# Opening and first sweep of a gated recurrence block: loads in written order, three products of the first unit over six row pairs first, side work tied to its units

## The chip, the cores and the metric

The kernel runs on one core of one Trainium2 chip. The metric is device time in microseconds (us) for one execution, lower is better. The engines are named as in the profile: PE (matrix products), PEld (its weight loads), DVE (vector), ACT (scalar), POOL (GpSimd), SP (the engine that issues most loads).

## What is computed

The block works on 1024 positions of 2048 channels. A conditioning vector gives a shift, a scale and a gate for each channel; the normalised input, scaled and shifted, is projected to eight parts (`w_in`) and to two merge gates (`w_merge`); a recurrence and a short convolution use the parts; two up-projections, a merge and a last projection follow.

```python
mod = jnp.einsum('bd,de->be', silu(c), w_ada[l]) + b_ada[l]
shift, scale, gate = (m[:, None, :] for m in jnp.split(mod, 3, axis=-1))
h = rms_norm(x, g_pre[l]) * (1.0 + scale) + shift
proj = jnp.einsum('bsd,de->bse', h, w_in[l])            # 8 parts of 1024 columns
...
merge = jax.nn.sigmoid(jnp.einsum('bsd,de->bse', h, w_merge[l]) + b_merge[l])
out = jnp.einsum('bsd,de->bse', m_a * p_a + m_b * p_b, w_o[l])
x = x + gate * rms_norm(out, g_post[l])
```

All weights and activations are 32-bit floats.

## The kernel before

**Products.** Each large product is made by a seven-product scheme over 2 x 2 blocks (p1 to p7), and each factor is split in a high and a low part, so that one row pair `g` of one product costs three matmuls of 128x128 by 128x512 (L118, L121, L122 in `mm3`). One product over eight row pairs is 24 matmuls. The split of a weight block is one ACT cast (`w_hi`, L129) and one DVE subtraction (`w_lo`, L130); that of an activation block is the same on half the size (L134, L135).

**Opening (`ph0`).** Sixteen loads bring x, the rows are normalised and transposed on PE into `xT` (L204). Then `ada_pair(q)`, for q from 0 to 3, forms shift and scale of 512 channels each: eight steps of two 512 KB loads, one of the scale weights that PE multiplies (`prow`, L234, two fp32 matmuls for each load, which the profile shows as four records) and one of the shift weights that DVE accumulates (`row_v`, L236 and L238). Every third of these 64 loads lands in a ring of four buffers of its own (`ada`), the others in the large pool `big` (38 slots of 4 KB per partition). At the end of each q, PE turns the two rows into columns (`pa`, L243), and DVE makes `a_c` and `sh_c` of them (L246 to L248). `factors_a` applies them to `xT` for two row pairs at a time and writes the split factors `fa` of p1, p6, p2 and p7. Row pairs 6 and 7 need the columns of q = 3, so they come last.

**First sweep (`ph1`).** 48 units; a unit loads four weight blocks (`w_raw`, 512 KB each, a ring of five buffers shared with scratch of the opening), forms s1, s2 and s4 on DVE, stores s1 and s4 to `s_scr`, and runs the four products p1, p6, p2, p7: 96 matmuls. Its result `o` is stored to `u_scr`. Unit 0 runs p1 and p6 over row pairs 0 to 5 first, in an order written out by hand (L341 to L344). Beside the units run three kinds of side work that no product of this sweep needs: `factors_b` (factors of the second sweep, written after units 0, 2 .. 14), `gate_step` (the gate's 32 loads and its accumulation on DVE, after units 16 to 31) and `sums_o` (sums of blocks of `w_o`, four loads, four DVE operations and four stores each, after units 32, 34 .. 46).

**Order.** Apart from what is pinned by hand, a planner at compile time sets the order in which each engine issues its instructions: it simulates the program and hands an engine, whenever that is free, the earliest written instruction that is ready by its own times and has a buffer. On the chip that order is fixed, and each engine and each load queue goes through it one by one. `keep_in_program_order` ties an instruction behind the one written before it on the same engine. `issue_after` ties what is written in its block, on the engine of a given instruction, behind that one. A pool opened after another one is closed lies in the same memory; its tiles wait for the old tiles at their place.

Of the kernel before, what the change touches and what calls it, by code (L numbers as in the profile page):

```python
# [15 lines left out]
P = 128  # L16
# [10 lines left out]
def tile_hgrn2_shortconv_block(  # L27
# [105 lines left out]
    def split_h(t, raw, eng):  # L133
        eng(out=t[:, 0], in_=raw)  # L134
        nc.vector.tensor_sub(out=t[:, 1], in0=raw, in1=t[:, 0].bitcast(F32))  # L135
# [40 lines left out]
    def load_x(si):  # L176
        for q in range(2):
            t = bigt(F32, f"x_{si}_{q}")
            nc.sync.dma_start(out=t, in_=x[si * P:(si + 1) * P, q * S:(q + 1) * S])
# [75 lines left out]
    def factors_a(gs, vec=()):  # L255
# [14 lines left out]
        def keep_f(s, g, raw):  # L270
            fa[s][g] = pair(f"f{s}_{g}")
            split_h(fa[s][g], raw, nc.scalar.copy)
# [9 lines left out]
        for g, b11, b12, b21, b22 in parts:  # L282
            keep_f("p7", g, b12)
# [15 lines left out]

    for si in range(8):  # L300
# [18 lines left out]
    units = [(w_in_v, (2 * j) * 1024 + i * P, (2 * j + 1) * 1024 + i * P) for i in range(NH) for j in range(4)]  # L319
    units += [(w_merge_v, 256 * m, 256 * m + P) for m in range(16)]  # L320

    def load_q(view, par, e0):
        raw = wp.tile([P, 8, P], F32, tag="raw", name="w_raw", bufs=5)
        nc.sync.dma_start(out=raw, in_=view[:, par, :, e0:e0 + P])
        return raw

    def unit_a(u):
        view, e1, e2 = units[u]
        a11, a21 = load_q(view, 0, e1), load_q(view, 0, e2)
        a22, a12 = load_q(view, 1, e2), load_q(view, 1, e1)  # L330
        o = ph.tile([P, 3, HS], F32, tag="o", name="o", bufs=2)
        s1, s2, s4 = (ph.tile([P, 8, P], F32, tag=f"s{n}", name=f"s{n}") for n in (1, 2, 4))
        px, py = ps("mm", "px"), ps("mm", "py")
        w1 = split_w(a11)
        if u:
            product(px, w1, fa["p1"])
        nc.vector.tensor_add(out=s1, in0=a21, in1=a22)
        nc.vector.tensor_sub(out=s2, in0=s1, in1=a11)
        nc.gpsimd.dma_start(out=s_scr[u][:, 0], in_=s1.rearrange("p a b -> p (a b)"))
        w6 = split_w(s2)  # L340
        if u == 0:  # L341
            for gs in (range(6), (6, 7)):
                product(px, w1, fa["p1"], pin=True, gs=gs)
                product(py, w6, fa["p6"], pin=True, gs=gs)  # L344
        nc.scalar.copy(out=o[:, 2], in_=px)  # L345
        if u:
            product(py, w6, fa["p6"])
        nc.vector.tensor_add(out=o[:, 1], in0=o[:, 2], in1=py)
        nc.vector.tensor_sub(out=s4, in0=a12, in1=s2)
        nc.gpsimd.dma_start(out=s_scr[u][:, 1], in_=s4.rearrange("p a b -> p (a b)"))  # L350
        product(px, split_w(a12), fa["p2"], more=True)
        nc.scalar.copy(out=o[:, 0], in_=px)  # L352
        nc.vector.tensor_sub(out=a21, in0=a11, in1=a21)
        product(py, split_w(a21), fa["p7"], more=True)
        nc.vector.tensor_add(out=o[:, 2], in0=o[:, 2], in1=py)
# [588 lines left out]
```

## Time and profile before

| | us |
|---|---|
| median of 3 runs | 2783.63 (2783.16 to 2787.78) |
| the profiled execution | 2786.26 |
| its span, first to last instruction | 2784.6 |
| PE busy in it | 2670.7 (96%) |
| DVE busy | 1725.3 (62%) |
| ACT busy | 915.0 (33%) |

The profiled execution lies 2.63 us, a tenth of a per cent, above the median. A busy PE in this profile includes the pipelined overlap of matmuls, so the rate at which matmuls start says more than the busy share. Times in the rows are us from the start of the span, unless marked ns.

### The profile page before, as it was taken

To read this page: it belongs to the slowest core of one execution; us is meant where nothing else is said; L and a number is where in the kernel's file an instruction comes from. 1 tells how busy PE (TensorE), PEld (TensorE's weight loads), DVE (VectorE), ACT (ScalarE), POOL (GpSimd) and SP (SyncE) were. 2 spreads that over 40 slices of the span, in tenths; PEclk is the share of its full clock that TensorE was granted. 3 is DMA by queue.
4 is the path that set the end of the run, shared out by engine and by line. 5 is a ranking of instruction groups with operands and counts; after the bars stand their busy time and mean duration, and the time that the engine had idled before them with its cause. 6 is when DMAs were issued, how large, how long until landed. Compare 5 with 4: busy or idle time off the path is not lost.

```text
span 2784.6 us, 31067 instructions
## 1 busy us (share of the span) xinstructions
PE 2670.7 (96%) x11851; PEld 2152.5 (77%) x11851; DVE 1725.3 (62%) x2128; ACT 915.0 (33%) x1192; POOL 246.6 (9%) x431
## 2 busy tenths in 40 slices
PE   4899999999999999999999999999998999999997
PEld 3277787888888888888888878888886877878785
DVE  6887886755544455546565666653338678755668
ACT  4433222222222222234334444333334232232334
POOL 2011111110000000020000000000001101000000
PEclk9999999999999999999999999999999999999999
DMA  9769999985555556683433443357665547673254
GB/s 361 282 229 324 317 356 356 347 279 183 190 181 174 177 173 192 184 299 124 142 124 122 142 139 123 119 190 228 201 225 175 173 148 248 221 272 99 85 213 171
DMA packets 405990, 576.76 MB, mean 207 GB/s; under 512 B 17772, under 2 KB 280016, under 8 KB 405712
## 3 DMA queue, kind: packets, MB, share of 16 engines
q1 hardware_dynamic: 352640, 369.15, 43.0%
q0 software_dynamic: 52016, 201.42, 19.0%
q10 hardware_dynamic: 1184, 4.20, 0.4%
q8 instruction: 93, 1.52, 0.2%
q14 instruction: 57, 0.47, 0.0%
HBM read 405.87 MB, written 168.82 MB: 206 GB/s over the span
## 4 chain that ended last, share of the span: by engine, by line
PE 71%; issue 11%; DVE 7%; DMA 6%; ACT 3%; POOL 2%; DVEq 0%; POOLq 0%; ACTq 0%; SPq 0%
PE po L833 9%; PE py L122 6%; PE py L121 6%; PE px L122 6%; PE py L118 6%; PE px L118 6%; PE px L121 6%; PE pz L118 5%; PE pz L122 5%; PE pz L121 5%; PE pw L121 3%; PE pw L122 3%; PE pw L118 3%; DMA w_raw<-in_w_in_dram 2%; DVE w_lo L130 1%
## 5 line engine op out<-in xcount | busy, mean ns | idle before, releaser
L129 ACT CAST w_hi<-w_raw 128x1024 fp32r<-128x1024 f32 (+1 forms) x304 | 299.4, 985 | 1008.7 <-PE px L121 401.3
L130 DVE TENSOR_TENSOR w_lo<-w_raw,w_hi 128x1024 fp32r<-128x1024 f32 (+1 forms) x304 | 345.3, 1136 | 260.4 <-ACT w_hi L129 256.3
L122 PE MATMUL py<-fp,w_lo 128*128 128x512 f32 x768 | 302.4, 394 | 7.2 <-DVE w_lo L130 7.1
L122 PE MATMUL px<-fp,w_lo 128*128 128x512 f32 x768 | 300.3, 391 | 5.5 <-DVE w_lo L130 5.5
L118 PE MATMUL py<-fp,w_hi 128*128 128x512 f32 x768 | 300.9, 392 | 2.2 <-ACT o L352 1.3
L118 PE MATMUL px<-fp,w_hi 128*128 128x512 f32 x768 | 300.5, 391 | 0.5 <-ACT o L345 0.5
L121 PE MATMUL py<-fp,w_hi 128*128 128x512 f32 x768 | 300.6, 391 | 0.0
L121 PE MATMUL px<-fp,w_hi 128*128 128x512 f32 x768 | 299.5, 390 | 0.0
L833 PE MATMUL po<-w_hi,lt 128*128 128x512 f32 x896 | 244.7, 390 | 6.2 <-ACT lt L134 4.0
L833 PEld LDWEIGHTS po<-w_hi,lt 128*128 128x128 f32 x896 | 167.9, 188 | 44.1 <-ACT lt L134 4.8
L122 PEld LDWEIGHTS py<-fp,w_lo 128*128 128x128 f32 x768 | 145.3, 189 | 42.6 <-DVE w_lo L130 12.1
L129 ACT CAST w_hi<-s 128x512 fp32r<-128x512 f32 (+1 forms) x112 | 90.2, 805 | 267.9 <-PE py L121 242.4
L122 PEld LDWEIGHTS px<-fp,w_lo 128*128 128x128 f32 x768 | 144.4, 188 | 37.1 <-DVE w_lo L130 7.0
L118 PEld LDWEIGHTS py<-fp,w_hi 128*128 128x128 f32 x768 | 145.2, 189 | 33.0 <-ACT w_hi L129 3.0
L118 PEld LDWEIGHTS px<-fp,w_hi 128*128 128x128 f32 x768 | 144.6, 188 | 31.7 <-ACT o L345 0.9
L121 PEld LDWEIGHTS py<-fp,w_hi 128*128 128x128 f32 x768 | 145.2, 189 | 30.4
L121 PEld LDWEIGHTS px<-fp,w_hi 128*128 128x128 f32 x768 | 144.6, 188 | 30.5 <-issue 0.5
L118 PE MATMUL pz<-fp,hi 128*128 128x512 f32 x384 | 151.8, 395 | 0.0
L121 PE MATMUL pw<-fp,w_hi 128*128 128x512 f32 x384 | 151.4, 394 | 0.0
L118 PE MATMUL pw<-fp,w_hi 128*128 128x512 f32 x384 | 151.0, 393 | 0.0
L118 PE MATMUL pz<-fp,w_hi 128*128 128x512 f32 x384 | 150.4, 392 | 0.0
L122 PE MATMUL pw<-fp,w_lo 128*128 128x512 f32 x384 | 150.1, 391 | 0.0
(285 smaller groups left out, 4917.2 us busy)
## 6 DMA issues: line engine op xcount, KB each, us to landing
w_raw<-in_w_in_dram SPq DMA_DIRECT2D x160, 512.0 KB, 5.1
s_scr<-s POOLq DMA_DIRECT2D x96, 512.0 KB, 6.0
s_raw<-s_scr SPq DMA_DIRECT2D x96, 512.0 KB, 4.2
w_raw<-in_w_merge_dram SPq DMA_DIRECT2D x80, 512.0 KB, 5.7
u_scr<-o POOLq DMA_DIRECT2D x48, 768.0 KB, 7.4
ada_raw<-in_w_ada_dram SPq DMA_DIRECT2D x64, 512.0 KB, 10.8
d<-u_scr SPq DMA_DIRECT2D x48, 512.0 KB, 5.0
ga_raw<-in_w_ada_dram SPq DMA_DIRECT2D x32, 512.0 KB, 8.4
```

What stands on the lines that cost most here:

```text
L118: mm = nc.tensor.matmul(o, ah, bh, start=first, stop=False, skip_group_check=True)
L121: nc.tensor.matmul(o, ah, bl, start=False, stop=False, skip_group_check=True)
L122: nc.tensor.matmul(o, al, bh, start=False, stop=last, skip_group_check=True)
L129: nc.scalar.copy(out=hi, in_=raw)
L130: nc.vector.tensor_sub(out=lo, in0=raw, in1=hi.bitcast(F32))
L833: nc.tensor.matmul(o, a, b[:, c], start=st, stop=sp, skip_group_check=True)
```

## The change

All loads of the opening and the first sweep are issued in written order (`load`). The ring of the conditioning loads shrinks: every fifth of them, instead of every third, goes to a buffer of its own, and there is one such buffer instead of four; the others go to `big`. Unit 0 moves into the opening's pool: its four weight loads are written before those of q = 3, its splits and s1, s2 too (a generator that stops at `yield`), and a third split (p2's) joins them. After the last `ada_pair` and `factors_a`, its products p1, p6 and p2 run over row pairs 0 to 5 and then over 6 and 7, in written order, p2 in a PSUM tile of its own; its remaining DVE work is tied behind the last factor. Side work is written after other units: `factors_b` after units 2, 4 .. 16, `gate_step` after 10 to 25, `sums_o` after 26, 28 .. 40.

```diff
+    def load(o, i):
+        tc.keep_in_program_order(nc.sync.dma_start(out=o, in_=i))
...
-        if n_ada[0] % 3:
+        if n_ada[0] % 5:
             raw = bigt(F32, "ada_raw").rearrange("p (k e) -> p k e", k=2)
         else:
-            raw = ph.tile([P, 2, HS], F32, tag="ada", name="ada_raw", bufs=4)
-        nc.sync.dma_start(out=raw, in_=w_ada_v[:, k:k + 2, t, q * HS:(q + 1) * HS])
+            raw = ph.tile([P, 2, HS], F32, tag="ada", name="ada_raw", bufs=1)
+        load(raw, w_ada_v[:, k:k + 2, t, q * HS:(q + 1) * HS])
...
-        row_p, row_v = (ph.tile([P, HS], F32, tag=t, name=t) for t in ("row_p", "row_v"))
+        row_p, row_v = (ph.tile([P, HS], F32, tag=t, name=t, bufs=n) for t, n in (("row_p", 1), ("row_v", 2)))
...
+    def load_a(u):
+        view, e1, e2 = units[u]
+        return [load_q(view, *a) for a in ((0, e1), (0, e2), (1, e2), (1, e1))]
+
+    def unit_a(u, raws):
+        a11, a21, a22, a12 = raws
+        o = ph.tile([P, 3, HS], F32, tag="o", name="o", bufs=2 if u else 1)
+        s1, s2 = (ph.tile([P, 8, P], F32, tag=f"s{n}", name=f"s{n}", bufs=1) for n in (1, 2))
+        s4 = ph.tile([P, 8, P], F32, tag="s4", name="s4") if u else a22
+        px, py = ps("mm", "px"), ps("mm", "py")
+        v = nc.vector
+        w1 = split_w(a11)
+        if u:
+            product(px, w1, fa["p1"])
+        v.tensor_add(out=s1, in0=a21, in1=a22)
+        v.tensor_sub(out=s2, in0=s1, in1=a11)
+        nc.gpsimd.dma_start(out=s_scr[u][:, 0], in_=s1.rearrange("p a b -> p (a b)"))
+        w6 = split_w(s2)
+        if u == 0:
+            w2 = split_w(a12, out_t=(ph.tile([P, 8, P], F32R, name="hi3a", bufs=1), wp.tile([P, 8, P], F32R, tag="raw", name="lo3a", bufs=5)))
+            yield
+            p2 = ps("mm", "p2")
+            for gs in (range(6), (6, 7)):
+                for p, w, f in ((px, w1, "p1"), (py, w6, "p6"), (p2, w2, "p2")):
+                    product(p, w, fa[f], pin=True, gs=gs)
+        nc.scalar.copy(out=o[:, 2], in_=px)
...
     for q in range(1, 4):
+        if q == 3:
+            first = unit_a(0, load_a(0))
+            next(first)
         ada_pair(q)
         factors_a((2 * q - 2, 2 * q - 1))
-    factors_a((6, 7), vec=(7,))
+    with tc.issue_after(factors_a((6, 7), vec=(7,)).ins):
+        next(first, None)
     ph_pool.__exit__(None, None, None)
...
     for u in range(NU):
-        unit_a(u)
-        if u < 16:
-            if u % 2 == 0:
-                factors_b(u // 2)
-        elif u < 32:
-            gate_step(2 * u - 32)
-            gate_step(2 * u - 31)
-        elif u % 2 == 0:
-            sums_o((u - 32) // 2)
+        if u:
+            for _ in unit_a(u, load_a(u)):
+                pass
+        if u in range(2, 18, 2):
+            factors_b(u // 2 - 1)
+        if 10 <= u < 26:
+            gate_step(2 * u - 20)
+            gate_step(2 * u - 19)
+        elif u in range(26, 42, 2):
+            sums_o((u - 26) // 2)
```

The loads in `load_x`, `gate_step` and `sums_o` go through `load` as well. The second sweep's `load_q` stays unpinned.

## Rows read from the trace of the kernel before

**Rows 1.** The page, part 1: busy us (share of the span) and instructions.
```profile
PE 2670.7 (96%) x11851; PEld 2152.5 (77%) x11851; DVE 1725.3 (62%) x2128; ACT 915.0 (33%) x1192; POOL 246.6 (9%) x431
```

**Rows 2.** Stretches: length; PE, PEld, DVE, ACT, POOL busy (instructions); clock share; DMA share; GB/s.
```profile
108.00:138.13 30.13, 23.34 (x73) 7.10 (x73) 27.62 (x45) 14.08 (x22) 0.00 (x0) 0.94 0.82 304
138.13:169.05 30.92, 25.93 (x98) 19.86 (x98) 26.80 (x36) 12.60 (x19) 2.73 (x5) 0.89 0.56 168
190.00:250.00 60.00, 56.35 (x248) 46.02 (x247) 50.22 (x63) 23.02 (x33) 11.74 (x22) 1.00 0.86 292
250.00:500.00 250.00, 243.30 (x1048) 198.26 (x1047) 188.88 (x207) 58.09 (x69) 37.59 (x70) 0.99 1.02 344
600.00:1212.00 612.00, 611.82 (x2693) 504.07 (x2692) 299.39 (x277) 144.97 (x168) 52.33 (x98) 1.00 0.61 187
```

**Rows 3.** Timeline of PE in the opening: start, length, what, [idle before <-releaser].
```profile
44.68 12.18 PE L234 MATMUL prow<-ada_raw,c_act 128*1 128x512 f32 x28
71.99 3.27 PE L234 MATMUL prow<-ada_raw,c_act 128*1 128x512 f32 x4 [15.13 <-DMA ada_raw<-in_w_ada_dram]
...
137.21 1.05 PE L243 MATMUL pa<-ones,row_v 128*128 128x1 f32 x8
138.13 0.49 PE L118 MATMUL px<-fp,w_hi 128*128 128x512 f32 x1
```

**Rows 4.** Timeline of SP's load queue in the opening, merged by line.
```profile
0.81 14.42 SPq L179 DMA_DIRECT2D x<-in_x_dram  x16
...
24.53 9.92 SPq L324 DMA_DIRECT2D w_raw<-in_w_in_dram  x5
34.50 89.07 SPq L223 DMA_DIRECT2D ada_raw<-in_w_ada_dram  x60
```

**Rows 5.** DMA, 0 to 140 us in 40 slices; adaLN loads of 40 to 140 us.
```profile
GB/s 123 305 386 414 411 410 406 387 340 291 285 365 379 392 387 386 387 387 387 386 386 149 225 150 92 208 273 373 365 394 387 386 389 387 385 386 387 240 0 5
...
DMA to landing us min/median/max: 3.8/10.8/12.0
```

**Rows 6.** Timeline of DVE from the last conditioning step to the last factor.
```profile
135.62 1.54 DVE L238 SCALAR_TENSOR_TENSOR row_v<-ada_raw,c_act,row_v 128x512 f32<-128x512 f32 x2
...
141.98 0.81 DVE L265 TENSOR_SCALAR xT<-xT,a_c,sh_c 128x1024 f32<-128x1024 f32 x1
...
150.18 1.28 DVE L278 TENSOR_TENSOR xT<-xT 128x512 f32<-128x512 f32 x2
...
160.67 0.69 DVE L135 TENSOR_TENSOR fp<-xT,fp 128x512 fp32r<-128x512 f32 x1
```

**Rows 7.** Timeline of PE inside unit 0 and at its end.
```profile
147.22 0.80 PE L122 MATMUL py<-fp,w_lo 128*128 128x512 f32 x1 [3.07 <-DVE w_lo L130]
147.82 0.63 PE L118 MATMUL py<-fp,w_hi 128*128 128x512 f32 x1
148.24 0.63 PE L121 MATMUL py<-fp,w_hi 128*128 128x512 f32 x1
...
169.05 0.39 PE L118 MATMUL px<-fp,w_hi 128*128 128x512 f32 x1
```

**Rows 8.** Two stalls of PE in the sweep and what DVE did before them.
```profile
220.10 0.68 DVE L291 TENSOR_TENSOR xx<-fp 128x512 f32<-128x512 f32 x1
...
222.57 0.50 PE L122 MATMUL py<-fp,w_lo 128*128 128x512 f32 x1 [2.12 <-DVE w_lo L130]
...
270.04 1.23 DVE L337 TENSOR_TENSOR s<-w_raw 128x1024 f32<-128x1024 f32 x1 [3.17 <-DMA w_raw<-in_w_in_dram]
...
274.85 0.50 PE L122 MATMUL px<-fp,w_lo 128*128 128x512 f32 x1 [2.99 <-DVE w_lo L130]
```

**Rows 9.** DMA issues: KB each, median us to landing; 250 to 400, 600 to 1200, page.
```profile
w_raw<-in_w_in_dram SPq DMA_DIRECT2D x25, 512.0 KB, 8.0
...
w_raw<-in_w_in_dram SPq DMA_DIRECT2D x42, 512.0 KB, 4.5
...
u_scr<-o POOLq DMA_DIRECT2D x48, 768.0 KB, 7.4
```

More of the change, by code (lines that the diff above doesn't have):

```diff
@@ L134, in split_h @@
         eng(out=t[:, 0], in_=raw)
-        nc.vector.tensor_sub(out=t[:, 1], in0=raw, in1=t[:, 0].bitcast(F32))
+        return nc.vector.tensor_sub(out=t[:, 1], in0=raw, in1=t[:, 0].bitcast(F32))
     STAGES = ("p1", "p6", "p2", "p7", "p5", "p4", "p3")
@@ L178, in load_x @@
             t = bigt(F32, f"x_{si}_{q}")
-            nc.sync.dma_start(out=t, in_=x[si * P:(si + 1) * P, q * S:(q + 1) * S])
+            load(t, x[si * P:(si + 1) * P, q * S:(q + 1) * S])
             xrow[si][q] = t
@@ L271, in keep_f @@
             fa[s][g] = pair(f"f{s}_{g}")
-            split_h(fa[s][g], raw, nc.scalar.copy)
+            return split_h(fa[s][g], raw, nc.scalar.copy)
         for g, b11, b12, b21, b22 in parts:
@@ L282, in factors_a @@
         for g, b11, b12, b21, b22 in parts:
-            keep_f("p7", g, b12)
+            last = keep_f("p7", g, b12)
+        return last
     def factors_b(g):
@@ L298, in factors_b, with load_q @@
             nc.gpsimd.dma_start(out=hb_scr[n][g], in_=t.rearrange("p a b -> p (a b)").bitcast(F32))
+    units = [(w_in_v, (2 * j) * 1024 + i * P, (2 * j + 1) * 1024 + i * P) for i in range(NH) for j in range(4)]
+    units += [(w_merge_v, 256 * m, 256 * m + P) for m in range(16)]
+    def load_q(view, par, e0, pin=True):
+        raw = wp.tile([P, 8, P], F32, tag="raw", name="w_raw", bufs=5)
+        (load if pin else nc.sync.dma_start)(raw, view[:, par, :, e0:e0 + P])
+        return raw
+    def load_a(u):
+        view, e1, e2 = units[u]
+        return [load_q(view, *a) for a in ((0, e1), (0, e2), (1, e2), (1, e1))]
@@ new lines, in unit_a @@
+    def unit_a(u, raws):
[21 more added lines that the diff above has]
+        if u:
+            product(py, w6, fa["p6"])
+        v.tensor_add(out=o[:, 1], in0=o[:, 2], in1=py)
+        v.tensor_sub(out=s4, in0=a12, in1=s2)
+        nc.gpsimd.dma_start(out=s_scr[u][:, 1], in_=s4.rearrange("p a b -> p (a b)"))
+        if u:
+            product(px, split_w(a12), fa["p2"], more=True)
+            nc.scalar.copy(out=o[:, 0], in_=px)
+        else:
+            v.tensor_add(out=o[:, 0], in0=o[:, 2], in1=p2)
+        v.tensor_sub(out=a21, in0=a11, in1=a21)
+        product(py, split_w(a21), fa["p7"], more=True)
+        v.tensor_add(out=o[:, 2], in0=o[:, 2], in1=py)
+        nc.gpsimd.dma_start(out=u_scr[u], in_=o)
@@ L317, in tile_hgrn2_shortconv_block @@
     ph = ph_pool.__enter__()
[L319 to L355, printed above, removed]
-        nc.gpsimd.dma_start(out=u_scr[u], in_=o)
     gacc = [None]
@@ L363, in gate_step @@
         raw = bigt(F32, "ga_raw").rearrange("p (k e) -> p k e", k=2)
-        nc.sync.dma_start(out=raw, in_=w_ada_v[:, 2 * kq:2 * kq + 2, 2, eb * HS:(eb + 1) * HS])
+        load(raw, w_ada_v[:, 2 * kq:2 * kq + 2, 2, eb * HS:(eb + 1) * HS])
         if kq == 0:
@@ L389, in sums_o @@
         for t, par, c in ((b12, 0, 1), (b22, 1, 1), (b11, 0, 0), (b21, 1, 0)):
-            nc.sync.dma_start(out=t, in_=w_o_v[:, par, g, :, c, :])
+            load(t, w_o_v[:, par, g, :, c, :])
         v = nc.vector
@@ L399, in tile_hgrn2_shortconv_block @@
     for u in range(NU):
-        unit_a(u)
-        if u < 16:
-            if u % 2 == 0:
-                factors_b(u // 2)
-        elif u < 32:
-            gate_step(2 * u - 32)
-            gate_step(2 * u - 31)
-        elif u % 2 == 0:
-            sums_o((u - 32) // 2)
+        if u:
+            for _ in unit_a(u, load_a(u)):
[7 more added lines that the diff above has]
+            sums_o((u - 26) // 2)
     ph_pool.__exit__(None, None, None)
@@ L430, in load_b @@
         nc.sync.dma_start(out=s1.rearrange("p a b -> p (a b)"), in_=s_scr[u][:, 0])
-        a22 = load_q(view, 1, e2)
+        a22 = load_q(view, 1, e2, pin=False)
         d1, d2 = bigt(F32, "d1"), bigt(F32, "d2")
```

## The prediction

> **What bounds the kernel now.** I read the page first: PE is busy 96% of the span [rows 1], so only time in which PE starts no matmul, or starts them slowly, can be won. The table of stretches shows where that is. From 600 to 1212 us the sweep runs 2693 matmuls in 612 us, 0.2273 us each [rows 2]; that is its steady rate, and a unit of 96 then takes 21.8 us. At this rate nothing is left to gain, and the change cannot make a matmul cheaper. Against it I hold the three stretches that the change touches. The opening lasts until 138.13 us, when the first product starts [rows 3]. Unit 0 ends at 169.05 us [rows 7], 30.92 us after its start, 9.1 us more than 21.8. In 250 to 500 us PE starts 1048 matmuls where the steady rate gives 1100, so 52 x 0.2273 = 11.8 us are lost; in 190 to 250 us it starts 248 instead of 264, which is 3.6 us [rows 2]. What lies behind 1213 us is not edited. The whole that could be won is thus the 25 us of the sweep and whatever the opening holds.
>
> **The opening: what limits it.** It moves 16 loads of x, 64 of the conditioning weights (60 of them in one run) and 5 weight blocks of the units, 512 KB each [rows 4], and the transfers run at 386 GB/s for most of it [rows 5], 1.36 us a load. There is one large hole: slices 22 to 27 (73 to 94 us) hold 149, 225, 150, 92, 208 and 273 GB/s; at 387 they would have held 2322, so (2322 - 1097) / 387 x 3.5 us = 11.1 us are lost [rows 5]. Its cause is order: PE stands still for 15.13 us before 71.99 us for one load of the first group [rows 3], while loads of the next group were brought ahead of it and filled the buffers. Written order removes this hole.
>
> **But the new ring makes a hole of its own.** Load 5 of the 64 lands in the single buffer, so load 10 cannot be issued before PE has used load 5, and in written order nothing can pass load 10. PE takes the conditioning products after the last transposes, from 44.68 us; 28 records in 12.18 us are seven loads (four records each), 1.74 us a load [rows 3]. Load 5 is the third that PE uses, so it is free at 44.68 + 3 x 1.74 = 49.9 us. A load into an idle queue lands 3.8 us later [rows 5], at 53.7. Loads 1 to 9 and x are 25 x 0.524 = 13.1 MB; summing the slices of 3.5 us gives 9.95 MB by 28 us, and the rest at 387 GB/s takes 8.1 us: they are in by 36.1 us [rows 5]. So the queue idles for 53.7 - 1.36 - 36.1 = 16.2 us. After that, a reuse every five loads has 5 x 1.36 = 6.8 us; 3.8 us of it is the landing, and 3.0 us are left for the use of the buffer, which takes 1.74 us on PE or 1.54 us on DVE [rows 3, 6]. That fits with 1.2 us to spare. The 54 loads behind load 10 take 73.3 us. Unit 0's four weight blocks now lie among them; slices 9 to 11 of before, where such blocks were moved, run at 285 to 340 GB/s; the slowest gives 1.84 us each [rows 5], 7.4 us. The last load lands at 53.7 + 73.3 + 7.4 = 134.4 us. Two accumulations on DVE (1.54 us [rows 6]) and the turning on PE (1.05 us [rows 3]) and their handovers end near 138 us. Before it was 138.13. I book 0 for the opening: one hole is traded for another. The bounds: no hole at all if PE takes the first conditioning products in the gaps ahead of its transposes, which gives up to 13 us (some of the 16 is eaten by DVE, which is busy 27.62 of the 30.13 us up to the first product already [rows 2]); and 6 us lost, if half of the ten further reuses come 1.2 us too late.
>
> The Trainium skill ("DMA: Bandwidth & Descriptors", Specifications) states a limit of about 358 GB/s of HBM for one core. By that a load of 512 KB takes 1.46 us, and the 54 loads would end 5.7 us later; this case's trace disagrees, with slices at 385 to 389 GB/s, and the sum stays with the trace.
>
> **Unit 0.** What goes: p6 no longer waits for its split. In before, the split of s2 ran on DVE after the opening; PE waited 3.07 us for its `w_lo` and then started matmuls 0.42 us apart [rows 7] where 0.2273 is steady, the lower of the clock's two levels (1.2 of 2.4 GHz); 0.89 of the clock was granted over the stretch [rows 2]. What is added: 18 products of p2 over row pairs 0 to 5 stand ahead of row pairs 6 and 7, so PE has 54 matmuls, 12.3 us, to cover the last factors. Those cost DVE, from the rows and their equals: the columns 0.5 us; L265 three times, 0.81 + 0.54 + 0.54; four pairs of splits at 1.3 us; L277 and L278 at 1.28 us for two; together some 10 us [rows 6]. In before they were mixed with the weight work of units 0 and 1 and ended at 161.3 us, 23 us after the columns [rows 6]; now `issue_after` keeps unit 0's rest behind them. 10 us lie inside 12.3 us, so the 96 matmuls run through, 21.8 us: 9.1 us won. If the cover fails, the loss is the overhang of DVE.
>
> What is late next is unit 1. Its first block can be loaded only when a buffer of the ring is free, after s4 (about 12 us after the first product), and lands 4.5 to 5 us later [rows 9]; with 2.3 us of splitting that is 19 us, before the 21.8 us are over. Its s1 is worse: it is a tile of the new pool. Laid out in order of first use, s1 lies at 12 to 16 KB, and unit 0's `o` at 10 to 16 KB of the old pool (row_p 2, row_v 4, ada 4, o 6 KB). Then it waits for the store of unit 0's `o`, 7.4 us [rows 9] and 1.2 us of addition and issue after the last product, and for 4.8 us of s1, s2 and splitting: p6 of unit 1 would start 13.4 us after unit 0 ends, with 5.4 us of p1 as cover (8 us lost), or 10.9 us if p2 goes first (2.5 us). Bounds 0 and 8; I take 3, near the case with p2 first, since the planner hands PE what is ready. Unit 0 and its follow-up give +6 us, between +1 and +9.
>
> **Side work.** In 250 to 500 us the queue is full: 344 GB/s, share 1.02, because gate and `w_o` loads are issued as soon as buffers allow. A weight block then lands in 8.0 us instead of 4.5 [rows 9]; DVE stands 3.17 us before s1, and PE 2.99 us behind it [rows 8]. Pinned behind the loads of units 10 to 40, the same 64 loads and 32 stores spread over some 30 units of 21.8 us, where the queue stands at a share of 0.61 [rows 2]. The gate's four fp32 products lie there and stay: at 0.87 us each, half of 1.74, they take 3.5 us and count as eight records or 1.8 us, so 1.7 of the 11.8 us is theirs and 10 can go; I leave 2 for new small stalls: +8, between +3 and +13. SP's queue now holds the next unit's blocks behind a gate or `w_o` load that waits for a slot; I price that at nothing, because once `factors_b` has freed its slots six are free and each set is asked for 43 us apart, and at up to 3 us for each stall like that of [rows 8] if not. `factors_b` has no load to hold it, so the planner may still place it early; its DVE work before the stall at 222.57 us [rows 8] stays, and I book 0 of the 3.6 us.
>
> **Sum.** 0 + 6 + 8 = 14 us. The profiled execution would take 2786.3 - 14 = 2772.3 us; the median lies 2.6 below it, so 2769.5 us.
>
> **Rivals.**
> - *The early hole doesn't open.* PE takes the products of loads 1 to 5 ahead of the last transposes, the transfers run on, and 13 us more are won: about 2757. For it: the first loads are in well before 44.68 us, at 1.36 us each. Against it: in before, where as early loads existed, PE took none ahead of 44.68 us [rows 3].
> - *Little comes of it.* The store of `o` costs its 8 us, the planner leaves stalls of other kinds in the sweep, and the opening loses 2 to 3 us: 2778 to 2785.
> - *Slower: the single buffer paces the whole opening.* Ten reuses after load 10; each is free as long as its use ends within 3.0 us of landing. Beyond that, lateness adds up one to one, since nothing passes in the queue. DVE works 27.62 of 30.13 us at the end of the opening [rows 2] and now also has five weight operations of 1.23 us there (L337's [rows 8]); 2 us too late at each costs 20 us, more than the 14 won: 2790. It decides from 1.4 us of lateness each.
> - *The clock.* With loads spaced 2.7 us apart on PE for 1.74 us of work, unit 0 could begin at the lower level, 0.42 us apart as from 147.82 us [rows 7]; over some 14 matmuls, as many as 5.7 us of that spacing hold, it costs 2.8 us: 2772. In before the first product followed the same kind of feed at the full clock, as far as its 0.49 us at 138.13 us shows [rows 3], so I hold it small. Its time lies inside the forecast's own range.
>
> The Trainium skill ("TensorE: Matmul & The Clock Gate", What's actually happening) says that the lower level is the default and that activity lifts it. By that rule the sparsely fed opening would hand unit 0 the lower clock; the trace shows the lower spacing only behind the stall at 147.22 us.
>
> **How the numbers follow.** Forecast 0.47 (2760 to 2778); the same with the lower clock 0.10; no early hole 0.14; little 0.19; slower 0.10. For 8 in 10 the range reaches from 2752, the first rival with a good sweep, to 2786. A difference of 0.2%, 5.6 us, is about what can be told from no change. Faster: 0.47 + 0.10 + 0.14 = 0.71, less 0.01 for the forecast's edge; same 0.19, the case of little; slower the rest, 0.11.
>
> **What would show it.** In the profile after: a hole in the transfers from about 36 to 52 us and none at 73 to 94; first product at 138 +- 3 us; 72 products of unit 0 without a gap and 96 in some 22 us; a wait before p6 or p2 of unit 1; 600 to 1100 us carrying the side work at the same 0.2273 us. Wrong would be: a first product before 130 or after 143 us, or stalls of PE behind pinned loads in units 10 to 40.

## The result and the profile after

The kernel became slower: 2865.64 us (median of 4, 2861.94 to 2869.98) against 2785.56 us (median of 4) on the same chip, a ratio of 1.0288, 95% interval 1.0266 to 1.0310. Forecast were 2769.5 us and a range that ended at 2786. The profiled execution took 2869.98 us, the slowest of the four, with a span of 2868.2. Lines of `kernel.py` have moved: what was L118 to L135 before (products and splits) is four higher now, the same holds for the conditioning steps (L234 to L243), L119 is the helper that issues a load, and L328 (L337 before) adds two weight blocks to `s`.

The page's line of busy times answers to [rows 1]: PE does the same 11851 instructions with the same work, and its share falls to 94%.

```profile
span 2868.2 us, 31015 instructions
PE 2704.3 (94%) x11851; PEld 2159.8 (75%) x11851; DVE 1726.2 (60%) x2129; ACT 914.2 (32%) x1191; POOL 246.7 (9%) x431
```

The table of stretches answers to [rows 2], cut here at the stages of the change: end of the opening, unit 0, units 1 to 9, 10 to 25 (gate), 26 to 41 (the `w_o` sums), 42 to 47. Columns: length; PE, PEld, DVE, ACT, POOL busy (instructions); granted clock; DMA share; GB/s.

```profile
108.00:147.00 39.00, 23.81 (x69) 7.50 (x69) 31.28 (x47) 16.46 (x24) 0.60 (x1) 0.90 0.87 295
147.00:183.85 36.85, 25.09 (x97) 19.86 (x98) 22.82 (x37) 12.03 (x18) 2.67 (x5) 0.82 0.46 150
183.85:389.56 205.71, 201.63 (x865) 165.08 (x865) 118.36 (x121) 52.63 (x66) 21.32 (x40) 0.98 0.66 215
389.56:785.53 395.97, 364.21 (x1546) 292.81 (x1544) 233.16 (x253) 87.74 (x106) 39.21 (x73) 0.98 0.68 227
785.53:1141.72 356.19, 340.14 (x1441) 272.27 (x1440) 194.24 (x178) 77.57 (x91) 42.22 (x79) 0.98 0.79 260
1141.72:1294.40 152.68, 152.68 (x673) 125.91 (x672) 71.27 (x66) 36.22 (x42) 18.74 (x35) 1.00 0.65 205
```

Only the last stretch runs at the steady rate, 673 matmuls in 152.68 us, 0.2269 us each. The two stretches with the held side loads (issued in written order, so that nothing passes them in SP's queue) do not: units 10 to 25 take 396 us for 16 units, 24.7 us each, though the transfers there are far from full (share 0.68).

For what follows I cut every trace the same way: a unit lasts from its first product to that of the next. The undisturbed units take 21.76 us in all kernels; the table gives the time above that, summed over units, with the first product and the start of the second sweep. Behind that start all kernels here need 1571 to 1574 us, so the table holds the differences.

```
               first   excess over 21.76 us in units      second
             product     0    1-9  10-25  26-41  42-47     sweep
before         138.1   9.2   14.3    4.7    1.8    0.2    1212.8
after          147.0  15.1    9.9   47.8   29.8    0.4    1294.4
side_free      146.0  14.3   18.3    5.7    2.7    0.6    1232.1
old_places     141.8  14.3    4.9   27.6   35.8   16.7    1285.7
gate_noadd     141.7  14.6    5.8   12.6   26.0    0.6    1245.8
tied           144.5  14.5    7.2   26.4   27.5    1.8    1266.4
late           142.0  14.4    7.0   97.7   62.1    6.5    1374.2
sums_noadd     142.8  14.6    5.9   41.5   25.2    0.5    1275.0
sums_halves    142.5  14.3    7.6   47.3   33.7    1.2    1291.2
swap           142.9  14.4    4.7   11.7   96.3    0.6    1315.0
ada_big        133.0  14.2    9.1   43.0   26.0    0.3    1270.1
fb_tied        141.2   2.1   10.1  115.9   24.9    0.2    1338.8
all_fixed      133.3   3.3    5.5   90.2   23.5    1.1    1301.4
free_all       133.7   3.3    5.8   98.6    1.3    0.3    1287.5
fb_early       131.7   1.8   16.5   16.4    2.5    1.0    1214.3
free_big       134.0  15.3   14.0    4.6    2.2    0.7    1215.3
fb_one         133.4   3.4   17.3    6.5    3.0    0.7    1208.7
```

Before to after, the start of the second sweep moves by 81.6 us: 8.9 from the opening, 5.9 from unit 0, -4.4 from units 1 to 9, 43.1 from units 10 to 25, 28.0 from units 26 to 41. The kernels with the opening of after put the first product anywhere from 141.2 to 147.0 us, so some 6 us of that column vary between them without any edit there.

What PE and DVE wait for in these stretches (total us, times, longest), which answers to [rows 8]. First PE from 183 to 1290 us, then DVE from 389 to 786 and from 786 to 1142 us:

```profile
PE px L126 <- DVE w_lo L134: 36.9, 20, 3.6
PE py L126 <- DVE w_lo L134: 10.0, 13, 2.2
```
```profile
DVE s L328 <- DMA w_raw<-in_w_in_dram: 68.5, 16, 6.2
DVE gacc L392 <- DMA ga_raw<-in_w_ada_dram: 41.5, 19, 3.8
```
```profile
DVE s L328 <- DMA w_raw<-in_w_merge_dram: 57.7, 10, 6.6
DVE wo L411 <- DMA wo<-in_w_o_dram: 27.0, 7, 5.7
```

PE waits for weight splits, and DVE, which makes them, stands in front of gate additions whose loads have not landed: 41.5 us in 19 waits. One such stall on the timeline (start, length, what, [idle before <- releaser]):

```profile
445.91 1.06 ACT L133 CAST w_hi<-w_raw 128x1024 fp32r<-128x1024 f32 x1 [4.38 <-PE px L125]
450.44 0.75 DVE L392 SCALAR_TENSOR_TENSOR gacc<-ga_raw,c_act,gacc 128x512 f32<-128x512 f32 x1 [2.32 <-DMA ga_raw<-in_w_ada_dram]
451.11 0.69 DVE L298 TENSOR_TENSOR xx<-xx 128x512 f32<-128x512 f32 x1
451.71 1.22 DVE L134 TENSOR_TENSOR w_lo<-w_raw,w_hi 128x1024 fp32r<-128x1024 f32 x1
452.99 0.50 PE L126 MATMUL px<-fp,w_lo 128*128 128x512 f32 x1 [0.99 <-DVE w_lo L134]
```

DVE idles for 2.32 us with work behind it that could run: L298 needs no load, and the cast of the split at 451.71 had ended at 446.97. The split comes late, and PE stands. This is the picture of the gate units; whether it is their cause is for the experiments.

### The profile page after: what moved, and what is told of

Its sections match the earlier page's. It is cut to its first block, busy times and chain, and to the rows that moved or that the text cites. A ratio compares the mean times of both kernels' runs of the same rounds, so it can differ in the third digit from the quotient of the medians.

```text
span 2868.2 us, 31015 instructions
## 1 busy us (share of the span) xinstructions
PE 2704.3 (94%) x11851; PEld 2159.8 (75%) x11851; DVE 1726.2 (60%) x2129; ACT 914.2 (32%) x1191; POOL 246.7 (9%) x431
## 3 DMA queue, kind: packets, MB, share of 16 engines
q0 software_dynamic: 52016, 201.42, 18.3%
## 4 chain that ended last, share of the span: by engine, by line
PE 57%; DMA 16%; issue 11%; DVE 10%; ACT 4%; POOL 1%; SPq 1%; DVEq 0%; POOLq 0%; ACTq 0%
PE po L853 9%; PE pz L122 5%; PE pz L126 5%; PE pz L125 5%; PE px L126 4%; PE px L122 4%; PE px L125 4%; DMA ga_raw<-in_w_ada_dram 4%; PE py L126 3%; PE py L122 3%; PE py L125 3%; DVE w_lo L134 3%; DMA w_raw<-in_w_in_dram 3%; DMA wo<-in_w_o_dram 3%; PE pw L125 3%
## 5 line engine op out<-in xcount | busy, mean ns | idle before, releaser
L122 PE MATMUL px<-fp,w_hi 128*128 128x512 f32 x760 | 303.4, 399 | 11.7 <-ACT w_hi L133 11.7
L328 DVE TENSOR_TENSOR s<-w_raw 128x1024 f32<-128x1024 f32 x48 | 58.8, 1225 | 203.4 <-DMA w_raw<-in_w_in_dram 121.7
```

What stands on the lines that cost most here:

```text
L328: v.tensor_add(out=s1, in0=a21, in1=a22)
```

## Experiments

My first theory: DVE's order is fixed, the additions of gate and sums stand close behind loads that are now issued late, and everything behind them on DVE waits (Q in the expectations). The rivals: the held loads stand ahead of the next unit's weight blocks in SP's queue and in the transfers, so that blocks land later (T); or the work costs this much because of the units that it was moved to. A time given below without a ratio is that of one execution; the four of after lie 8 us apart.

### Which part costs the sweep its time

Gate's additions left out, loads in place:

```diff
             k = 2 * kq + j
+            if k > 0:
+                continue
```

> The changed kernel with the gate's accumulation left out: of the 64 additions on DVE for the gate only the four that begin a column block stay (so the gate is not the reference's); all its 32 loads stay where they are in SP's written order. Changed kernel: 2865.6 us; units 10 to 25 (369 to 743 us of its span) hold about 45 us of lost matmul starts. Theory Q (DVE goes through a fixed order, and the gate's additions stand in it ahead of a weight block's w_lo while their own load has only just been issued): without the additions nothing waits, and units 10 to 25 run at 21.8 us each; total near 2825. Theory T (the side loads hold up the weight blocks behind them in SP's queue or in the transfers): loads unchanged, so the stalls stay, total 2858 to 2866.

Measured: 2818.47 us (kernel before beside it 2779.13). Units 10 to 25 fall from 47.8 to 12.6 us, with the same 32 loads at the same places; units 26 to 41 keep 26.0. The additions, not the bytes, cost 35 of the 43 us. DVE's largest wait, the one for weight blocks, is still there, no smaller than the 68.5 us above, and costs little in these units (DVE from 389 to 786 us):

```profile
DVE s L328 <- DMA w_raw<-in_w_in_dram: 79.2, 17, 6.1
```

Nor does the additions' own work on DVE explain it: `side_free`, below, does the same 64 additions in units 3 to 9 and loses 24.0 us in units 1 to 25, where after loses 57.7 and `gate_noadd`, almost without them, 18.4. The additions could cost this in two ways, by DVE's order or by keeping the loads' slots. SP decides it: in after, from 385 to 790 us, no load waits for a slot of the large pool; these are all its waits of over 1 us in total:

```profile
SPq L119 <- DVE w_lo L134: 262.1, 49, 10.0
SPq L119 <- DMA w_raw<-in_w_in_dram: 74.9, 17, 6.9
SPq L119 <- DVE s L328: 21.6, 16, 1.7
```

They are waits for the weight blocks' own ring. So Q holds for the gate.

The loads of gate and `w_o` not held:

```diff
-        load(raw, w_ada_v[:, 2 * kq:2 * kq + 2, 2, eb * HS:(eb + 1) * HS])
+        nc.sync.dma_start(out=raw, in_=w_ada_v[:, 2 * kq:2 * kq + 2, 2, eb * HS:(eb + 1) * HS])
...
-            load(t, w_o_v[:, par, g, :, c, :])
+            nc.sync.dma_start(out=t, in_=w_o_v[:, par, g, :, c, :])
```

> The changed kernel, only gate and w_o loads no longer pinned (the weight blocks still are), so that the planner may issue them as early as buffers allow, as in the kernel before. Theory Q: their loads run far ahead of their additions again; the sweep loses what it lost before, 10 to 15 us, and what stays is the opening's 9 us and unit 0's 15 us: total 2800 to 2812. If the time came from where the side work is written and not from the pin: about 2865.

Measured: 2805.12 us. Units 10 to 41 fall from 77.6 to 8.4 us. The planner brings the loads forward again, to 231 to 569 us, and there the queue is full again, as in [rows 2], at 1.03 of its share, and a weight block lands in 9.1 us (median). Stretch 380 to 570 us of this kernel, the last 70 us of it alone, and the weight loads of the whole stretch (KB each, median us to landing):

```profile
380.00:570.00 190.00, 185.67 (x813) 151.80 (x812) 131.17 (x125) 42.93 (x50) 30.09 (x57) 1.00 1.03 352
500.00:570.00 70.00, 70.00 (x311) 57.95 (x310) 47.50 (x44) 16.42 (x19) 10.32 (x20) 1.00 1.02 339
w_raw<-in_w_in_dram SPq DMA_DIRECT2D x35, 512.0 KB, 9.1
```

813 records of PE in 190 us are 3% short of the steady rate, and the 5.7 us that units 10 to 25 lose lie in units 10 and 11, up to about 445 us. From 500 to 570 us the queue is as full and PE runs at the steady rate: a full queue alone does not stall PE. That it does was the premise of my +8 us. Earlier, while the gate's additions are under way (239 to 395 us), PE does lose time (18.3 us in units 1 to 9, 14.3 before); the run does not part the queue from the additions there.

Gate and sums back at the units of before, all loads held:

```diff
-        if u in range(2, 18, 2):
-            factors_b(u // 2 - 1)
-        if 10 <= u < 26:
...
-        elif u in range(26, 42, 2):
+        if u < 16:
+            if u % 2 == 0:
+                factors_b(u // 2)
+        elif u < 32:
...
+        elif u % 2 == 0:
```

> The changed kernel with the side work written after the units of the kernel before (factors_b after 0 to 14, gate after 16 to 31, w_o sums after 32 to 46), all loads still pinned. Theories Q and T: the same stalls a few units later, 2860 to 2870. If the places were the cause: about 2805.

Measured: 2861.84 us. The stalls move with the work (units 42 to 47 now lose 16.7) and their sum stays. The hold is the cause, then, and not the choice of these units rather than those of before.

### Can held loads be made harmless by later uses?

The uses (additions, sums and stores) tied behind the end of the same unit on DVE (`tied`, below), or of the unit behind it (`late`, the same with the tie one unit on); `ends[u]` holds the last addition of unit u on DVE and its last copy on ACT:

```diff
-            gate_step(2 * u - 20)
-            gate_step(2 * u - 19)
+            ns = (2 * u - 20, 2 * u - 19)
+            raws = [gate_load(n) for n in ns]
+            with tc.issue_after(ends[u][0]):
+                for n, raw in zip(ns, raws):
+                    gate_add(n, raw)
...
```

> The changed kernel, with the gate's additions and the sums of w_o of a unit tied on DVE behind that unit's last addition, so some 20 us behind the issue of their loads and not a whole unit later as in the run before, which held more buffers than there are; loads, places and amount of work as in the changed kernel. Theory Q (the fixed order on DVE: a use right behind its load): units 10 to 41 lose 10 to 20 us instead of 80; total 2795 to 2805. Theory T (the pinned loads hold up the weight blocks) and theory W (too much DVE work in a unit): no change, 2862 to 2870.

> The changed kernel with all loads in the same written order, but the gate's additions and the sums of w_o that use a load are written, and tied on DVE, behind the end of the next unit: the same work and the same loads, only no use right behind its load. Theory Q: the waits of DVE for gate and w_o loads go, about 70 us of the stalls in units 10 to 41 with them; total near 2795 to 2805. Theory T: 2865, as the queue of loads is the same. Theory W (there is simply too much DVE work in a unit): 2865 too.

Measured: `tied` 2840.02 us, ratio 1.0189 (1.0164 to 1.0215), between the theories; `late` 2947.9 us, worse than anything. DVE's waits for gate loads are no longer among its five longest in `tied` (380 to 786 us), yet units 10 to 25 still lose 26.4 us, in units 13, 15 and 17 above all (22 us). What SP's queue stands in front of says why, first in `tied` (380 to 640 us), then in `late` (whole span):

```profile
SPq L119 <- DVE fb L139: 52.6, 4, 30.8
SPq L119 <- DVE w_lo L134: 48.5, 16, 7.0
SPq L119 <- DVE gacc L398: 47.5, 3, 21.5
```
```profile
SPq L119 <- DVE gacc L398: 196.4, 16, 42.4
```

Now a held load does wait for a slot of the large pool, up to 42.4 us, and all weight blocks of the next unit wait behind it. Held loads leave a choice of two costs: with early uses DVE waits for the loads, with late ones the loads wait for slots.

### The sums: bytes, additions or place

`sums_noadd` leaves out the four additions of sums_o; `sums_halves` splits a set's loads over two units (only its call is shown):

```diff
-        v.tensor_sub(out=b22, in0=b22, in1=b12)
-        v.tensor_sub(out=b12, in0=b12, in1=b11)
-        v.tensor_add(out=b11, in0=b22, in1=b11)
-        v.tensor_sub(out=b21, in0=b11, in1=b21)
```
```diff
-        elif u in range(26, 42, 2):
-            sums_o((u - 26) // 2)
+        elif u in range(26, 42):
+            sums_o((u - 26) // 2, u % 2)
```

> The changed kernel with sums_o's four additions on DVE left out (its loads stay at their held places and its stores move the blocks as loaded). In units 26 to 41 the changed kernel loses 29 us. Theory Q, the DVE's fixed order (additions placed right behind loads that have not landed, weight splits queued behind them): 29 falls below 10, time 2843 to 2848 us. Theory T, four held loads in a row ahead of the next unit's weight blocks, which then land later: 23 or more stay, time 2860 to 2870 us.

> The changed kernel with the four held w_o loads of a set split over two units: two loads behind each of units 26 to 41 instead of four behind every second; the same bytes, the same additions, nothing left out. Theory T (the burst in front of the weight blocks): a block then waits behind 1 MB instead of 2 MB, the loss of 29 us falls to between 8 and 15, time 2850 to 2858 us. Theory Q (DVE waits for the loads just issued): two waits in each unit instead of four in every second, no gain, 2863 to 2873 us.

Measured: 2849.07 and 2863.75 us; 25.2 and 33.7 us are lost in units 26 to 41. Without the additions nearly all of the loss stays, so DVE's waits for `wo` are not the cause here; halving the burst wins nothing, so T as I had put it falls too. The trace of `sums_noadd` shows what stands there instead. All five gaps of PE over 0.9 us from 770 to 1130 us come behind an `s` (L328) that waits 6.4 to 8.3 us for a block of `w_merge`; behind it on DVE stands a split whose cast had ended some 6 us earlier or, once, an addition that PE waits for. One of them (ACT, DVE and PE in order of time):

```profile
955.58 1.05 ACT L133 CAST w_hi<-w_raw 128x1024 fp32r<-128x1024 f32 x1 [4.38 <-PE px L125]
958.97 1.23 DVE L328 TENSOR_TENSOR s<-w_raw 128x1024 f32<-128x1024 f32 x1 [6.52 <-DMA w_raw<-in_w_merge_dram]
962.51 1.22 DVE L134 TENSOR_TENSOR w_lo<-w_raw,w_hi 128x1024 fp32r<-128x1024 f32 x1
963.78 0.50 PE L126 MATMUL px<-fp,w_lo 128*128 128x512 f32 x1 [2.12 <-DVE w_lo L134]
```

The blocks issued behind four `w_o` loads land in 11.8 to 14.9 us there (935 to 1000 us), in before in 4.6 to 6.9 in the same stretch. So the link through DVE's order is the same, but the late load is a weight block behind the held ones. This is read from the trace; no run tests it alone.

In all these kernels the loss sits in units 32 to 41 (after 26.1 us, against 3.7 in 26 to 31). From unit 32 on the blocks come from `w_merge`; their shape is the same, but in before, where no side loads run beside them, they land in 5.5 us (830 to 1140 us, median of 57), those of `w_in` in 4.5 (600 to 740 us, 25) (the next expectation has 5.2 and 4.2). So gate and sums were exchanged:

```diff
-        if 10 <= u < 26:
-            gate_step(2 * u - 20)
-            gate_step(2 * u - 19)
-        elif u in range(26, 42, 2):
-            sums_o((u - 26) // 2)
+        if 26 <= u < 42:
+            gate_step(2 * u - 52)
+            gate_step(2 * u - 51)
+        elif u in range(10, 26, 2):
+            sums_o((u - 10) // 2)
```

> The changed kernel with gate and sums_o in each other's places: sums_o behind units 10 to 24, gate behind units 26 to 41, all loads held as in the changed kernel, nothing left out. Theory M: the sets of four w_o loads hurt where the weight blocks come from w_merge (units 32 on, landing 5.2 us without side loads against 4.2 for w_in) and not elsewhere: units 10 to 25 then lose under 10 us in all, and units 32 to 41 with the gate's loads at least the 4 us a unit that gate cost before, 40 us or more; time 2840 to 2855 us. Theory B (the sets' bytes cost 4 us a set anywhere): units 10 to 25 lose 25 us or more, time 2865 us or more.

Measured: 2888.65 us. Units 10 to 25, now with the sums, lose 11.7 us, a little over the 10 expected and under half of what the sums' units lose in after; the gate's units lose 7.2 us each in 32 to 41 and 4.1 in 26 to 31, against 3.0 at their old place. So the same held work costs about twice as much, or more, where the blocks come from `w_merge`. The time itself was missed, since I had left the gate its old price. The stalls have the form of those in after, with longer waits: all nine gaps of PE over 4 us come behind a gate addition that waits 5.8 to 6.9 us for its load (DVE, 740 to 1140 us):

```profile
DVE gacc L392 <- DMA ga_raw<-in_w_ada_dram: 58.1, 13, 6.2
```

Whether the 1 us of landing is the reason stays open; no run changed it alone.

### The opening and unit 0

All conditioning loads in the large pool:

```diff
-        if n_ada[0] % 5:
+        if True:
```

> The changed kernel, with all 64 conditioning loads landing in the large pool, so that none waits for the one small buffer. If that buffer sets the opening: the hole in the transfers from 38 to 50 us and the one from 93 to 97 us close, the first product starts at 128 to 134 us instead of 142 to 147, total 2850 to 2857. If DVE or PE sets it: the first product stays at 138 to 147 us and the total within 5 us of 2865.

Measured: 2842.54 us, first product at 133.01 us. The transfers at 30 to 60 us (40 slices of 0.75 us, GB/s), after and then `ada_big`:

```profile
GB/s 393 388 388 377 388 377 385 385 158 44 0 0 0 0 0 0 0 0 0 0 0 0 0 0 0 79 240 330 418 385 380 385 404 385 393 393 391 385 382 393
```
```profile
GB/s 388 388 399 369 374 388 391 391 391 382 388 391 377 391 374 385 391 391 382 388 382 382 391 393 382 391 388 374 391 393 391 388 382 385 382 388 391 393 382 391
```

The single buffer makes the hole of some 13 us, and without it the opening ends 8 to 14 us earlier than with it.

`factors_b` tied behind the end of its unit on ACT and DVE:

```diff
         if u in range(2, 18, 2):
-            factors_b(u // 2 - 1)
+            with tc.issue_after(ends[u][1]), tc.issue_after(ends[u][0]):
+                factors_b(u // 2 - 1)
```

> The changed kernel, with the work of factors_b tied on ACT and DVE behind the end of the unit that it is written after (2, 4 .. 16), so that it can't stand ahead of unit 1's split. If PE's wait of 11.7 us at the end of unit 0 is ACT's queue (a cast of factors_b that waits for a store of its buffer, with unit 1's w_hi behind it): unit 0 and that wait together take 25 to 27 us instead of 37 to 45, total 2850 to 2856. If it is unit 1's tile s1 on unit 0's stored o, as the prediction had it: the wait stays, 2862 to 2868.

Measured: 2912.7 us, far above both expectations; unit 0 falls from 14 to 2.1 us above 21.76, and units 10 to 17 lose some 96 us, for held gate loads now wait for slots that `factors_b` still has (SP from 330 to 520 us):

```profile
SPq L119 <- DVE fb L139: 90.0, 2, 47.0
```

The first number says that `factors_b` held unit 0 up; the second repeats `late` with another holder of the slots.

### Putting the parts together

Four kernels combine these edits. `all_fixed` is tied uses, tied `factors_b` and the large pool; `free_all` is loads not held, tied `factors_b` and the large pool; `free_big` is loads not held and the large pool; `fb_early` is `free_all` with `factors_b` behind units 1 to 8.

> The three edits together (uses tied behind their unit, factors_b tied, conditioning loads all in the large pool) on the changed kernel. If the three causes add up and nothing new comes: 2865 - 65 - 11 - 11 = 2778, so equal to the kernel before or a little faster, 2765 to 2785. If the tied factors_b or the full pool meet the gate's buffers: 2790 to 2830.

> Three parts of the changed kernel altered together: all conditioning loads in the large pool (no single buffer), the gate and w_o loads no longer held to their written place, factors_b tied behind the end of its unit on ACT and DVE. In the run with the last two ties and held loads, units 10 to 16 lost 18 us each on SP waiting for slots. Theory 'held loads': those losses were the price of loads that could not be passed by the weight blocks, so they vanish here and the three gains add up: first product at 133 us, unit 0 within 3 us of 21.8, 10 to 20 us of stalls in the other 47 units, second sweep from 1191 to 1203 us, time 2762 to 2774 us, faster than the kernel before. Theory 'slots': factors_b at its late place simply keeps the six slots too long, whoever waits for them; then the gate loads come late but still on the path, and the time is 2830 to 2850 us.

> Two parts of the changed kernel altered: all conditioning loads in the large pool, and gate and w_o loads not held; factors_b as the change has it. Alone the second gave 2805.1 us with the first product at 146.0; the first gave a first product at 133.0. If the two add up: 2805.1 - 13 = 2792 us, within 4 us, unit 0 still 14 us over 21.8. If the opening's gain is given back in units 1 to 11 (the same loads meet the same slots 13 us sooner): 2800 to 2806 us.

> As the run with all conditioning loads in the large pool, unheld side loads and tied factors_b, but factors_b is tied behind units 1 to 8, one a unit, so that it has given back its slots before the first gate load is written. There SP stood 47 us at a time on factors_b's slots with gate loads (132 us in four waits) and units 10 to 17 lost 97 us. Theory 'slots held by late factors_b': those 97 us vanish; first product at 133.5 us, unit 0 about 3 us over 21.8, 10 to 25 us of stalls in the other units; second sweep from 1191 to 1206 us, time 2761 to 2777 us, faster than the kernel before. Theory 'tying is itself the cost' (ACT or DVE waits for factors_b's stores in the units where it is tied, now every unit): units 1 to 9 lose 5 us or more each, time 2790 us or more.

Measured: `all_fixed` 2879.47 us, ratio 1.0337 (1.0318 to 1.0355), and `free_all` 2861.01, 1.0277 (1.0260 to 1.0294): opening and unit 0 as hoped, and 90 and 99 us lost in units 10 to 25. I had expected `free_all` to be cured by letting the loads go. It was not: the planner itself places gate loads ahead of blocks at a time when, on the chip, `factors_b` still has the slots (SP from 330 to 560 us; L385 is the load of the gate there):

```profile
SPq L385 <- DVE fb L139: 89.5, 2, 47.0
```

So in these units the cost is not the hold by itself but a load that waits for a slot ahead of weight blocks; the hold is one way to get it. `free_big` gave 2788.24 us, ratio 1.0012 (1.0003 to 1.0021), the parts adding up as expected; `fb_early` 2789.23, 1.0012 (1.0002 to 1.0023): unit 0 is clear (1.8), the 99 us are gone, but units 1 to 25 lose 33 us instead of 19, and the 2761 to 2777 us expected were missed.

Last, only the first set of `factors_b` tied, behind unit 1:

```diff
+            if u <= 2:
+                with tc.issue_after(ends[1][1]), tc.issue_after(ends[1][0]):
+                    factors_b(u // 2 - 1)
...
```

> All conditioning loads in the large pool, gate and w_o loads not held, and of the eight sets of factors_b only the first is tied behind the end of unit 1 on ACT and DVE; the rest stay as the changed kernel has them. The same without the tie took 2788 us, with unit 0 15 us over 21.8 and 18 us of stalls in the other 47 units. If the first set's place in ACT's order is the whole cost of unit 0: unit 0 falls to 3 us over, units 1 to 11 stay at 18 to 22 us, time 2774 to 2780 us, faster than the kernel before by 0.2 to 0.4%. If the loss moves instead (the slots come free later, gate loads and splits meet them in units 1 to 11): 30 us there, time 2784 to 2792 us.

Measured: 2780.78 us against 2784.20, ratio 0.9986 (0.9976 to 0.9995), just above the 2774 to 2780 expected, and the only version faster than the kernel before, narrowly, by 0.14%. Unit 0 falls by 11.9 us, units 1 to 25 give 5 back. The first set was the cause in unit 0.

## Why the prediction was wrong, step by step

**The side work** was the step that failed: +8 us were booked and 71 were lost (43.1 and 28.0). The wait that I priced at nothing, SP's queue behind a load without a slot, is indeed not there in after; the six free slots were enough as long as the uses came early. What I did not price is that use. I spread the loads and left the additions on DVE out of the sum: they follow their loads at once, DVE takes its work in a fixed order, and a weight split that stands behind them makes PE wait. In the gate's units that costs 35 us (`gate_noadd`). In the `w_o` units the loss of 28.0 us comes from the hold (2.7 us are left in `side_free`) and hardly from the additions (`sums_noadd`); the trace shows late weight blocks in front of the splits there, and that part of the cause is not tested by itself. [rows 8] had the link, a DVE wait that becomes a PE stall, and up to 3 us was the right size of one: from 389 to 1142 us there are 41 gaps of PE over 0.3 us, 1.4 us each on average, 55.7 us in all. No rival had so many. Under what would be wrong stands "stalls of PE behind pinned loads in units 10 to 40", and that is what happened, as did a first product after 143 us.

The gain was overstated as well. I read the 11.8 us of [rows 2] as the price of a full queue. In `side_free` PE keeps the steady rate from 500 to 570 us at a share of 1.02 (above), and so does before itself, at 1.04:

```profile
500.00:570.00 70.00, 70.00 (x311) 57.97 (x310) 46.21 (x44) 16.59 (x19) 11.76 (x22) 1.00 1.04 353
```

Of the +8, the 4.4 us of units 1 to 9 came.

**The opening.** The hole was forecast from 36 to 52 us; it runs from about 36 to 51 in the slices above. Its mechanism was right: load 10 is issued at 47.95 us (49.9 forecast). The end was not: the last load lands at 140.81 us instead of 134.4, the first product starts at 147.00 instead of 138. A second hole opens at about 90.5 to 98 us (0.5 us a slice, 85 to 105 us):

```profile
GB/s 397 369 319 315 397 406 406 401 418 377 377 246 45 25 25 12 0 0 0 0 0 0 66 127 250 287 397 406 401 402 385 348 393 397 377 389 401 397 393 389
```

Load 40 is issued at 95.28 us only, when PE has used load 35 in the single buffer, and PE is late because the turning of the group before stands ahead of it, in two parts of 1.9 us, with 2.50 us of idle time ahead of the first:

```profile
84.83 1.86 PE L247 MATMUL pa<-ones,row_p 1*128 1x1 f32 x8 [2.50 <-ACT row_p L243]
86.63 3.57 PE L238 MATMUL prow<-ada_raw,c_act 128*1 128x512 f32 x4
90.13 1.87 PE L247 MATMUL pa<-ones,row_v 128*128 128x1 f32 x8
```

So the step "reuses fit with 1.2 us to spare" counted a product's own 1.74 us and not what stands ahead of it on PE. The rival of the single buffer had the pacing, though with DVE as the late engine, and I gave it 0.10. Behind the last load, DVE and PE need 6.2 us where I took 3.6: from 140.39 us on DVE has five splits to do among its accumulations (1.88 and 1.28 us), which the sum left out. They are the rest (last lines before the first product, compare [rows 3]):

```profile
139.57 1.88 PE L238 MATMUL prow<-ada_raw,c_act 128*1 128x512 f32 x4 [0.83 <-DMA ada_raw<-in_w_ada_dram]
142.11 1.05 PE L247 MATMUL pa<-ones,row_p 1*128 1x1 f32 x8 [0.66 <-ACT row_p L243]
145.64 1.50 PE L247 MATMUL pa<-ones,row_v 128*128 128x1 f32 x8 [2.48 <-DVE row_v L242]
147.00 0.77 PE L122 MATMUL px<-fp,w_hi 128*128 128x512 f32 x1
147.57 0.63 PE L125 MATMUL px<-fp,w_hi 128*128 128x512 f32 x1
148.00 0.63 PE L126 MATMUL px<-fp,w_lo 128*128 128x512 f32 x1
```

And the hole was worth less than I wrote: without it 133.0 us, 5 us before the kernel before, where I had put 13.

**The clock** was a rival of 2.8 us, held small. It came: the first 13 matmuls are 0.43 us apart, and the granted clock is the lower level, 1.2 of 2.4 GHz, at first (147 to 150 us; the lines above it show the end of the opening):

```profile
130.00:143.00 13.00, 9.01 (x26) 1.89 (x24) 11.65 (x19) 3.87 (x7) 0.00 (x0) 1.00 0.76 280
143.00:147.00 4.00, 1.52 (x10) 1.44 (x10) 2.55 (x4) 0.00 (x0) 0.00 (x0) 0.88 0.00 0
147.00:150.00 3.00, 3.00 (x8) 2.42 (x9) 2.79 (x8) 2.43 (x3) 0.00 (x0) 0.50 0.02 5
```

That is 13 x 0.20 = 2.6 us; in before the first product started at 0.49 us [rows 3]. What PE did before it: 3.1 us of idle time in the last 7 of the opening, in the lines above. From 130 to 143 us, mostly under the spaced feed that the rival blamed, the clock was still full (1.00); it fell between 143 and 147 us (0.88), where PE waits 2.48 us for the turning. The Trainium skill ("TensorE: Matmul & The Clock Gate", What's actually happening) has the lower level as the default that activity lifts; the trace agrees here.

**Unit 0** went as forecast up to its end. The 72 held products run without a gap and the 24 of p7 follow; the last starts at about 172 us, 25 us after the first, where before took 30.9 [rows 7], so 5.9 of the 9.1 us were won and the clock took 2.6. Unit 1's first block is issued at 158.43 us and lands at 163.17, as the prediction had it. Then comes a wait that it did not have. ACT (columns as above):

```profile
164.86 0.62 ACT L138 CAST fb<-xx 128x512 fp32r<-128x512 f32 x1
174.23 0.62 ACT L138 CAST fb<-xx 128x512 fp32r<-128x512 f32 x1 [8.75 <-DMA hb_scr<-fb]
175.60 0.62 ACT L138 CAST fb<-keep 128x512 fp32r<-128x512 f32 x1 [0.76 <-DVE fb L139]
182.23 0.62 ACT L138 CAST fb<-xx 128x512 fp32r<-128x512 f32 x1 [6.01 <-DMA hb_scr<-fb]
182.76 1.04 ACT L133 CAST w_hi<-w_raw 128x1024 fp32r<-128x1024 f32 x1
```

The planner put casts of `factors_b` ahead of unit 1's weight split; they wait 8.75 and 6.01 us for stores to give back slots, and the split of a block that has been there since 163.17 us runs at 182.76. PE stands for 11.7 us. Of `factors_b` I had written that "the planner may still place it early" and looked at its work on DVE alone; its stores, and what queues on ACT behind a cast that waits for one, were not counted. The wait for unit 0's `o`, my named rival, does not appear: tying the first set of `factors_b` alone took unit 0's excess from 15.3 to 3.4.

## What to carry to other kernels

A load that is held to its place has two prices: a use placed right behind it stops its engine for all that follows there, and a use placed later keeps the buffer, so that the next held load stops its queue; before holding one, name what queues behind the use and what frees the buffer. A full DMA queue is not itself a cost: see whether the engine at the bound ever waits behind it. When a part of a change is removed or tied, look for the slots it now keeps longer; gains of parts did not add up until no load waited for a slot.

## What the runs showed of the hardware

Blocks of 512 KB with the same shape land in 5.5 us from `w_merge` and in 4.5 us from `w_in` (medians of before, 57 and 25 loads, no side loads around). A stall costs PE more than its length: in `swap` from 740 to 1140 us PE loses 62.7 us in gaps and another 21.1 us in 106 matmuls that start 0.4 us apart behind them, and the granted clock of the stretch is 0.93:

```profile
740.00:1140.00 400.00, 344.03 (x1386) 275.42 (x1385) 196.03 (x207) 74.36 (x87) 30.70 (x57) 0.93 0.58 183
```

In the gate units of after the same two terms are 36.4 and about 7 us.
